# A hybrid encoder block: an SSM scan in three levels, the meta keys' low parts from PSUM, and a reordered end of the experts

## The chip, the cores and the metric

The kernel runs on one core of one Trainium2 chip. The metric is the device time of one execution, in microseconds (us). TensorE (PE) does the matrix products, VectorE (DVE) and ScalarE (ACT) the elementwise work, GpSimd (POOL) some of it too; SyncE (SP), ACT and POOL issue the transfers (DMAs).

## The reference, cut to what matters

One block over 2048 tokens and 16 meta tokens of 1024 values. Attention and a bidirectional state-space layer run side by side, are gated and summed; then come 16 experts that each choose 256 tokens.

```python
q, k, v, u, g_attn, g_ssm = split(layer_norm(concat(meta, x)) @ w_in)
# attention: softmax(q k^T / 8) v over all 2064 keys, 8 heads
# state-space layer, per direction (forward, backward):
s[t] = a * s[t-1] + B u[t]          # a, s complex; 32 groups of 64 states
y[t] = Re(C s[t]) + d * u[t]
y_ssm = glu(gelu(y))
h = layer_norm(alpha * h + (sig(g_attn) * (y_attn @ wa) + sig(g_ssm) * (y_ssm @ ws)) @ w_o)
# experts: each takes its top 256 tokens
moe[idx[e]] += gate[e] * ((silu(xe @ w_gate[e]) * (xe @ w_up[e])) @ w_down[e])
out = layer_norm(alpha * h + moe)
```

## The kernel before

Where precision asks for it, a float32 operand is split into a high part (a copy in a format that TensorE multiplies fast) and a low part (the rest), and a product is three products. The parts are made on the way: high by ACT, low by DVE or POOL.

**Order of the program.** `phase_a` normalises and projects q, k, v and u. Then `ssm` and `glu` run as generators: at each `yield` the driver (`drive`) takes so many steps from `gates`, whose step is four matmuls of 512 columns (L1169). So the gates' products fill TensorE while the state-space layer keeps the other engines busy, and every engine gets its instructions in the order in which the program writes them. A gate weight arrives as `gwr`, ACT makes `gwh`, DVE makes `gwl` (L1127), and the finished gate tile `pg` is read by ACT (L1140).

**`ssm`.** It first loads its parameters: raw `a` (L712), `log_dt` (L714), `c` (L720) and `b` (L724), all from SP's queue. `v_item` computes, per chunk of 16 time steps, what the chunk adds to the state, and ACT copies it to `VA`, a tile with 130 places of 64 values a partition. `scan` then walks over 127 places: five DVE instructions of 64 values for each (L675), the forward and the backward direction in one instruction, from two places of `VA`. Each step takes one gate step. Beside it `k_item` prepares the output weights of five groups; its elementwise instructions are on POOL here (L879, L881). `y_item` multiplies the states by these weights (L1013).

**Attention** goes over 32 units (four blocks of 512 queries by 8 heads). A unit has nine steps `i`: eight of 256 keys and the last, i = 8, of the 16 meta keys. In each step TensorE makes the scores `pS` (L483, L484), ACT the exponential `pe` (L490) and the high part `ph` (L502; for i = 3 DVE, L500), POOL the low part `pl` (L508), and TensorE the product with v (`po`, L525, L527). For the meta keys the low part is made by DVE (L511), from `pe` and `ph` in SBUF. TensorE also makes the scores of the next unit's maxima (`pm`, L449), two at a time, and DVE reduces each (`mx`, L455). After a block's eighth head POOL sends `y` to DRAM (L548).

**Experts.** Each has eight units of gate and up products (`pg`, L1721) and eight of down products (`pd`, L1749), with 24 matmuls of 256 columns in a down unit and 48 in a gate-and-up unit, 9216 in all for 16 experts. From expert 9 on (`E0`) side generators run one step per unit: `finish` normalises rows of the sum that no expert of the end touches, `redo(e - 1)` those of the expert before. `MO` holds their times: at which unit `redo` is started, how many units it waits, the same for the last expert's, and the pitch of `finish`. `norm` takes two row tiles: sums on ACT (L1810, L1816), Newton steps on DVE, then two DVE instructions of 1024 values per tile (L1821, L1822). `put_rows` (L1825) writes rows to the output.

Of the kernel before, what the change touches and what calls it, by code (L numbers as in the profile page):

```python
# [49 lines left out]
def kernel(ctx, tc, x, meta, ln_in_g, ln_in_b, w_in, q_norm_g, k_norm_g,  # L50
# [321 lines left out]
    def phase_b(c):  # L372
# [100 lines left out]
        def scores(n, i, a):  # L473
# [13 lines left out]
            e = pp.tile([128, 2, 512], F32, name="pe", bufs=PR["PE"])  # L487
# [5 lines left out]
        PR = dict(HI=(3,), LOV=(16,), LAG=4, LEAD=3.75, PE=7, PH=5, LOS=2,  # L493
# [98 lines left out]
        for s in range(len(steps) + LAG):  # L592
# [76 lines left out]
    def ssm(c):  # L669
# [7 lines left out]
        VA = tb.tile([128, 2, 32, CB + 2], F32, name="VA")  # L677
        PL.memset(VA[:, 1, :, CB:CB + 1], 0.0)
# [4 lines left out]
        st = tb.tile([128, 2, 2, 32], F32, name="st")  # L683
# [17 lines left out]
        with pool(name="s_i", bufs=1) as ti:  # L701
# [163 lines left out]
            do(V.tensor_scalar, lt[64:, 1], lt[64:, 1], -1.0, None, op0=OP.mult)  # L865
# [7 lines left out]
        up = c1.enter_context(pool(name="s_u", bufs=2))  # L873
        bstv = bst.rearrange("p r (d g) h -> p r d g h", d=2)
# [26 lines left out]

        def v_item(k, d, g):
# [15 lines left out]
            A.copy(VA[:, d, 4 * k + g, :CB], pv[:, :CB])  # L918

        load_u(0, True)  # L920
        make_ws(0)
        yield
        for i, _ in enumerate(pipe(v_item(k, d, g) for k in range(8) for d in range(2) for g in range(4))):
            yield (i + 1) % 2
        c1.close()
        c1 = ExitStack()
        kp = c1.enter_context(pool(name="s_k", bufs=1))
        up = c1.enter_context(pool(name="s_v", bufs=2))
        CL, MM = {}, {}
# [30 lines left out]
        def load_mm(k):  # L960
            mm = kp.tile([128, KT, 2, TH], F32, name="mm", bufs=3)
# [648 lines left out]
    def experts(c, pos, inf):  # L1610
# [446 lines left out]
```

## Time and profile before

| what | value |
|---|---|
| time, median of 3 runs | 3305.42 us (3301.82 to 3309.93) |
| time of the profiled execution | 3306.01 us |
| its span, first to last instruction | 3303.9 us |
| TensorE busy | 92% of the span |
| VectorE busy | 69% |
| ScalarE busy | 47% |
| GpSimd busy | 30% |
| mean granted TensorE clock | 0.966 |

The shares of busy time are means over stages that differ. By the stretches of the span: `phase_a` to 302 us, the state-space layer and gates to 966 us (its scan from 471.6 to 695), attention to 1650 us, merge, router and top-k to 2109 us, experts to the end. The granted clock is a share of full speed (2.4 GHz).

### The profile page before, as it was taken

The numbers are of one execution on the slowest core, as the hardware profiler recorded it, in microseconds if no ns is written. First come the engines' busy times: TensorE is split into PE (matmuls) and PEld (weight loads), VectorE is DVE, ScalarE is ACT, GpSimd is POOL, SyncE is SP. The second block draws the span as 40 slices with busy tenths as digits, with TensorE's granted clock in tenths as the row PEclk, the third lists the DMA queues.
The fourth block names the chain that finished last, engine by engine and source line by source line (L and its number), as shares of the span: only waits on it lengthen the run. The fifth ranks groups of instructions, "written<-read, shape, count | busy, mean of one in ns | idle before, by whom it ended". The sixth has DMA issues, their size and how long they took to land. (4 is left out here: it accounts for less than half of the span.)

```text
span 3303.9 us, 56603 instructions
## 1 busy us (share of the span) xinstructions
PE 3045.8 (92%) x22805; PEld 2686.9 (81%) x22805; DVE 2287.5 (69%) x4206; ACT 1557.3 (47%) x2197; POOL 1000.7 (30%) x633
## 2 busy tenths in 40 slices
PE   6999996788999999999999997599999999999997
PEld 5887785566777777777778886599999999999997
DVE  7884779985357777777556665666566665778875
ACT  2222341112349889898732222344444444556552
POOL 3221050033039989898820001000011001112221
PEclk9999998899999999999999998799999999999998
DMA  6666521544730101012086652366666666878773
GB/s 223 192 193 213 132 77 53 163 131 139 217 109 21 33 21 33 17 36 86 27 254 191 175 169 104 110 210 203 204 205 214 208 204 217 262 235 281 262 255 133
DMA packets 464502, 513.03 MB, mean 155 GB/s; under 512 B 47568, under 2 KB 387728, under 8 KB 463856
## 3 DMA queue, kind: packets, MB, share of 16 engines
q1 hardware_dynamic: 435104, 422.31, 40.4%
q0 software_dynamic: 19232, 69.53, 7.2%
q10 hardware_dynamic: 9904, 17.57, 1.5%
q8 instruction: 179, 2.93, 0.4%
q14 instruction: 83, 0.68, 0.1%
HBM read 385.59 MB, written 123.76 MB: 154 GB/s over the span
## 5 line engine op out<-in xcount | busy, mean ns | idle before, releaser
L1721 PE MATMUL pg<-xh,wh 128*128 128x256 f32 x2048 | 586.3, 286 | 15.7 <-DVE sg L1729 9.7
L1721 PE MATMUL pg<-xh,wl 128*128 128x256 f32 x2048 | 582.8, 285 | 0.5 <-DVE wl L1630 0.5
L1721 PE MATMUL pg<-xl,wh 128*128 128x256 f32 x2048 | 582.9, 285 | 0.0
L1630 DVE TENSOR_TENSOR wl<-wr,wh 128x2048 fp32r<-128x2048 f32 x189 | 433.1, 2292 | 215.1 <-ACT wh L1629 215.1
L508 POOL TENSOR_TENSOR pl<-pe,ph 128x1024 f16<-128x1024 f32 x256 | 554.6, 2201 | 79.7 <-DVE ph L500 67.1
L455 DVE TENSOR_REDUCE mx<-pm 128x1 f32<-128x412 f32 (+1 forms) x640 | 365.5, 584 | 153.6 <-PE pm L449 138.3
L1721 PEld LDWEIGHTS pg<-xh,wh 128*128 128x128 f32 x2048 | 396.6, 194 | 17.0 <-issue 12.2
L1721 PEld LDWEIGHTS pg<-xh,wl 128*128 128x128 f32 x2048 | 396.6, 194 | 0.7 <-DVE wl L1630 0.7
L1721 PEld LDWEIGHTS pg<-xl,wh 128*128 128x128 f32 x2048 | 396.8, 194 | 0.0
L1629 ACT CAST wh<-wr 128x2048 fp32r<-128x2048 f32 x189 | 358.4, 1896 | 7.3 <-DMA wr<-in_w_up_e_dram 5.7
L1169 PE MATMUL pg<-gh,gwh 128*128 128x512 f32 x1024 | 344.8, 412 | 12.9 <-ACT gg L1140 6.9
L490 ACT ACTIVATE pe<-pS,ebias 128x1024 f32<-128x1024 f32 (+1 forms) x288 | 306.6, 1065 | 63.3 <-PE pS L484 62.6
L1749 PE MATMUL pd<-wh,hh 128*128 128x256 f32 x1024 | 292.6, 286 | 5.2 <-ACT ye L1767 2.7
L1749 PE MATMUL pd<-wh,hl 128*128 128x256 f32 x1024 | 290.5, 284 | 0.7 <-DVE hl L1736 0.7
L1749 PE MATMUL pd<-wl,hh 128*128 128x256 f32 x1024 | 290.2, 283 | 0.0
L1169 PE MATMUL pg<-gh,gwl 128*128 128x512 f32 x512 | 213.0, 416 | 63.0 <-DVE gwl L1127 62.9
L449 PE MATMUL pm<-k,q 128*128 128x412 f32 (+1 forms) x640 | 237.7, 381 | 33.4 <-DVE mx L455 29.0
L502 ACT CAST ph<-pe 128x1024 f16<-128x1024 f32 (+1 forms) x256 | 254.2, 993 | 18.3
L1169 PEld LDWEIGHTS pg<-gh,gwh 128*128 128x128 f32 x1024 | 200.1, 198 | 59.8 <-ACT gg L1140 8.8
L525 PEld LDWEIGHTS <-ph 128*128 128x128 f16 (+1 forms) x2176 | 190.5, 97 | 65.0 <-issue 61.8
L525 PE MATMUL po<-v,ph 128*128 128x129 f16 (+1 forms) x2176 | 234.0, 222 | 0.7 <-ACT t L533 0.7
L483 PE MATMUL pS<-q,k 128*128 128x512 f32 (+1 forms) x544 | 232.7, 428 | 0.0
(412 smaller groups left out, 6848.7 us busy)
## 6 DMA issues: line engine op xcount, KB each, us to landing
wr<-in_w_gate_e_dram SPq DMA_DIRECT2D x64, 1024.0 KB
wr<-in_w_up_e_dram SPq DMA_DIRECT2D x64, 1024.0 KB
wr<-in_w_down_e_dram SPq DMA_DIRECT2D x64, 1024.0 KB
gwr<-in_w_in_dram SPq DMA_DIRECT2D x32, 512.0 KB
gh<-ht_d SPq DMA_DIRECT2D x64, 256.0 KB
gt_d<-gg ACTq DMA_DIRECT2D x64, 256.0 KB
gt<-gt_d SPq DMA_DIRECT2D x32, 512.0 KB
q<-q_d SPq DMA_DIRECT2D x96, 128.0 KB
```

The source lines that it names most:

```text
L449: PE.matmul(p[:, :w], Q[n][0][:, 128 * j:128 * j + 128], K1[units[n][1] // 4][:, k0:k0 + w], start=True, stop=True)
L455: V.tensor_reduce(MX[n][:, j, c:c + 1], p[:, :w], axis=AX.X, op=OP.max)
L483: PE.matmul(p[:m, a], K2[g][:, k0:k0 + m], Q[n][1], start=True, stop=False)
L490: A.activation(e[:m, :w], p[:m, :w], AF.Exp, bias=ebias[:m], scale=HD ** -0.5)
L502: A.copy(hi[:m, :w], e[:m, :w])
L508: PL.tensor_tensor(lo[:m, :w], e[:m, :w], hi[:m, :w], op=OP.subtract)
L525: PE.matmul(o[:, 0:129], hi[:m, a, 128 * j:128 * j + 128], v16[:m, kt, g, 0:129], start=(kt == 0 and j % 2 == 0), stop=False, skip_group_c ...
L1169: PE.matmul(p, w[:, k], h, start=(k == 0 and j == 0), stop=(k == 7 and j == 2))
L1629: A.copy(wh, wr)
L1630: V.tensor_tensor(wl, wr, f(wh), op=OP.subtract)
L1721: PE.matmul(p[:, gu], w[:, k, cs_], x[:, k], start=(k == 0 and j == 0), stop=(k == 7 and j == 2))
L1749: PE.matmul(p, a[:, k, cs_], w[:, k], start=(k == 0 and j == 0), stop=(k == 7 and j == 2))
```

## The change

Four parts of the program change.

1. **Attention.** For the meta keys the exponential is written to the free half of the score tile in PSUM (`p[:, 1:]`), and not to a tile in SBUF. DVE's low part reads that. It enters DVE's queue at the end of its own step i = 8, where before it came two steps later with POOL's.
2. **State-space layer.** Nine of the parameter loads are issued by ACT and not by SP. `VA` is laid out place by place, the backward direction in reverse order, so that both directions walk the same way; `powers` makes the first eight powers of `a`. `scan` has three levels: inside 16 segments of 8 places all segments at once (7 steps of 1024 values), then over the segments' ends (15 steps of 64 values), then the ends' contribution to the other places, three segments at once (5 steps of 1344 values). Its wide instructions take two gate steps each. `take_vs` copies a group's states to a contiguous tile for the products; `u` and `mm` of the output stage lie in pools that are opened when the scan is over.
3. **Experts' memory.** A pad of 32 bytes stands ahead of the experts' tiles and one of 64 bytes ahead of the token tiles `xh`, `xl`, which get a pool of their own.
4. **Experts' order.** 24 transposes of a constant stand ahead of the first gather's use. In the last seven experts `MO` is (2, 5, 5, 11), the two long DVE instructions of `norm` are a step apart, `finish` loads its next rows earlier, and the last expert's down units finish the first half of its rows earlier.

```diff
@@ attention
-            e = pp.tile([128, 2, 512], F32, name="pe", bufs=PR["PE"])
+            e = pp.tile([128, 2, 512], F32, name="pe", bufs=PR["PE"]) if w == 2 else p[:, 1:]
...
+        def split_lo(n, i):
             e, hi, lo, m, w = P[n, i]
...
+            (PL if w == 2 else V).tensor_tensor(lo[:m, :w], e[:m, :w], hi[:m, :w], op=OP.subtract)
...
-                vq += split_lo(*steps[s - PR["LOS"]], True)
+            if 0 <= s - PR["LOS"] < len(steps) and steps[s - PR["LOS"]][1] < NP - 1:
+                split_lo(*steps[s - PR["LOS"]])
...
                 split_hi(n, i, False)
+                if i == NP - 1:
+                    vq.insert(0, lambda st=steps[s]: split_lo(*st))
@@ ssm
-        VA = tb.tile([128, 2, 32, CB + 2], F32, name="VA")
+        VA = tb.tile([128, CB + 1, 2, 32], F32, name="VA")
...
-                    SP.dma_start(raw[:, i, j], src.rearrange("l d g p -> (l d g) p"))
+                    A.dma_start(raw[:, i, j], src.rearrange("l d g p -> (l d g) p"))
...
-            SP.dma_start(ldt, row_bcast(ssm_log_dt, DG))
+            A.dma_start(ldt, row_bcast(ssm_log_dt, DG))
...
-                    SP.dma_start(craw[:, :, x, y], src.rearrange("l d g h p -> (l d g h) p")
+                    A.dma_start(craw[:, :, x, y], src.rearrange("l d g h p -> (l d g h) p")
...
-            A.copy(VA[:, d, 4 * k + g, :CB], pv[:, :CB])
+            dst = VA[:, 1:, d, 4 * k + g]
+            A.copy(back(dst, CB) if d else dst, pv[:, :CB])
...
+        def take_vs(k):
+            VS[k] = yp.tile([128, 2, 2, CX], F32, name="vs", bufs=2)
+            for d in range(2):
+                src = VA[:, 1 - d:1 - d + CX, d, 2 * k:2 * k + 2]
+                A.copy(VS[k][:, d].rearrange("p g c -> p c g"), back(src, CX) if d else src)
...
-            for m in range(1, CB - 1):
-                f0, f1 = m - 1, m
-                b0, b1 = CB - m, CB - 1 - m
-                tt(st[:, 0], lt[:, 0], slot(f0, b0, 0, 128), OP.mult)
-                tt(st[:64, 1], lt[64:, 1], slot(f0, b0, 64, 128), OP.mult)
-                tt(st[64:, 1], lt[:64, 1], slot(f0, b0, 0, 64), OP.mult)
-                cur = slot(f1, b1, 0, 128)
-                tt(cur, cur, st[:, 0], OP.add)
-                tt(cur, cur, st[:, 1], OP.add)
+            for j in range(1, SL):
+                dims = [NS, 64]
+                coef = [wide(z[:, r, 0:1], dims) for r in range(2)]
+                for _ in step(coef, v[:, j - 1], v[:, j], dims):
+                    yield 2
+            for s in range(1, NS):
+                for _ in step([z[:, r, SL - 1] for r in range(2)], v[:, SL - 1, s - 1], v[:, SL - 1, s], [64]):
+                    pass
+                yield
+            B = 3
+            for s in range(1, NS, B):
+                dims = [B, SL - 1, 64]
+                coef = [wide(z[:, r, None, 0:SL - 1], dims) for r in range(2)]
+                prev = wide(v[:, SL - 1, s - 1:s - 1 + B, None], dims)
+                cur = v[:, 0:SL - 1, s:s + B].rearrange("p j s x -> p s j x")
+                for _ in step(coef, prev, cur, dims):
+                    yield 2
...
-        kk = pipe((k_item(k, False) for k in range(5)), every=22)
+        kk = pipe((k_item(k, False) for k in range(5)), every=12)
...
+        up = c1.enter_context(pool(name="s_v", bufs=2))
+        yp = c1.enter_context(pool(name="s_y", bufs=3))
@@ experts
+        c.enter_context(pool(name="e_pad", bufs=1)).tile([128, 8], F32, name="skew")
...
-        MO = dbg.get('MO', (2, 6, 3, 11)) if dbg else (2, 6, 3, 11)
+        MO = dbg.get('MO', (2, 5, 5, 11)) if dbg else (2, 5, 5, 11)
...
+        c.enter_context(pool(name="e_skew", bufs=1)).tile([128, 16], F32, name="skew")
+        tp = c.enter_context(pool(name="e_xt", bufs=2))
...
-                    put_rows(e, h)
+                    if h:
+                        put_rows(e, h)
...
                 V.scalar_tensor_tensor(x, x, mean[:, j:j + 1], gb, op0=OP.add, op1=OP.mult)
+                yield
                 V.scalar_tensor_tensor(x, x, r[:, j:j + 1], bb, op0=OP.mult, op1=OP.add)
...
-                yield from norm([xs[t], xs[t + 1]])
+                for n, _ in enumerate(norm([xs[t], xs[t + 1]])):
+                    if n == 7 and t + 2 < NT:
+                        load(t + 2)
+                        load(t + 3)
+                    yield
...
-            yield from norm(AC[e])
-            put_rows(e, 0)
-            yield
-            yield
+            for n, _ in enumerate(norm(AC[e])):
+                if n == 7:
+                    put_rows(e, 0)
+                yield
             put_rows(e, 1)
...
-        pick_out(0, pick(0))
+        pi = pick(0)
+        for _ in range(3):
+            p = pp.tile([128, 4, 128], F32, name="pt")
+            for k in range(8):
+                PE.transpose(p[:, k % 4], idf, idf)
+        pick_out(0, pi)
...
+            seq = [(i, h) for i in range(4) for h in range(2)]
+            if not more:
+                seq[4:] = [(2, 0), (3, 0), (2, 1), (3, 1)]
...
+        put_rows(E - 1, 0)
         run(post)
```

How the rows stand on the engines is seen at three places. On DVE, between two units of the attention, before (`mx` are the maxima, `nm` what is made of a unit's twenty, L511 the meta keys' low part):

```order
L464 TENSOR_REDUCE nm_8226<-m_8652 128x4
L455 TENSOR_REDUCE mx<-pm 128x1 x10
L511 TENSOR_TENSOR pl<-pe,ph 16x512
L455 TENSOR_REDUCE mx<-pm 128x1 x7
L500 TENSOR_REDUCE ph<-pe 128x1024
```

And with the change, where L506 is the same low part, read from the score tile in PSUM:

```order
L464 TENSOR_REDUCE nm_7900<-m_8286 128x4
L455 TENSOR_REDUCE mx<-pm 128x1 x8
L506 TENSOR_TENSOR pl<-pS,ph 16x512
L455 TENSOR_REDUCE mx<-pm 128x1 x9
L500 TENSOR_REDUCE ph<-pe 128x1024
```

The low part has moved ahead by two maxima, and its first operand is PSUM.

On DVE at the start of the scan, before (the last rows of the input weights `ws`, then the first two places of the scan; `gwl` belongs to the gates):

```order
L881 TENSOR_TENSOR ws<-ws,wt 128x1024
L675 TENSOR_TENSOR st<-lt,VA 128x64
L675 TENSOR_TENSOR st<-lt,VA 64x64 x2
L675 TENSOR_TENSOR VA<-VA,st 128x2x32 x2
L675 TENSOR_TENSOR st<-lt,VA 128x64
```

And with the change at the same place:

```order
L894 TENSOR_TENSOR ws<-ws,wt 128x1024
L1009 TENSOR_TENSOR st_5058<-pw,VA 128x1024
L1011 TENSOR_TENSOR st_5059<-pw,VA 64x1024
L1188 TENSOR_TENSOR gwl<-gwr,gwh 128x1024
L1013 TENSOR_TENSOR st_5059<-pw,VA 64x1024
L1015 TENSOR_TENSOR VA<-VA,st_5058 128x16x64
L1017 TENSOR_TENSOR VA<-VA,st_5059 128x16x64
L1009 TENSOR_TENSOR st_5125<-pw,VA 128x1024
```

635 short rows became 35 of 1024 values, 75 of 64 and 25 of 1344; the `gwl` rows, 11 before and 11 now, stand between the wide ones.

On ACT at the start of the state-space layer, before (L251 ends `phase_a`; L1140 reads a finished gate tile, L1141 sends it away):

```order
L251 CAST qh<-pk 128x16
L1140 ACT_TABLE_LOAD
L1140 ACTIVATE gg<-pg 128x512
L1141 DMA gt_d<-gg 128x512
L1140 ACTIVATE gg<-pg 128x512
```

And with the change:

```order
L251 CAST qh<-pk 128x16
L708 DMA s_3480<-in_ssm_a_re_dram 64x64 x2
L708 DMA s_3480<-in_ssm_a_im_dram 64x64 x2
L710 DMA s_3485<-in_ssm_log_dt_dram 128x64
L716 DMA s_3488<-in_ssm_c_re_dram 128x8x64
L716 DMA s_3488<-in_ssm_c_im_dram 128x8x64 x2
L716 DMA s_3488<-in_ssm_c_re_dram 128x8x64
L1201 ACT_TABLE_LOAD
L1201 ACTIVATE gg<-pg 128x512
```

The nine loads now stand ahead of ACT's first reading of a gate tile.

## Rows read from the trace of the kernel before

**Rows 1.** Windows: length, busy (count) PE, PEld, DVE, ACT, POOL, clock, DMA, GB/s

```profile
395.00:471.60 76.60, 76.34 (x530) 69.53 (x529) 58.68 (x51) 45.65 (x139) 25.74 (x31) 1.00 0.35 105
471.60:695.00 223.40, 158.12 (x595) 119.25 (x593) 205.65 (x656) 30.61 (x45) 28.91 (x24) 0.84 0.33 105
```

**Rows 2.** DVE's groups by line in the scan: busy us, mean ns, idle before

```profile
L675 DVE TENSOR_TENSOR st<-lt,VA 128x64 f32<-128x64 f32 x381 | 115.7, 304 | 19.9 <-ACT VA L918 10.5
L675 DVE TENSOR_TENSOR VA<-VA,st 128x64 f32<-128x64 f32 x254 | 76.7, 302 | 8.3
L1127 DVE TENSOR_TENSOR gwl<-gwr,gwh 128x1024 fp32r<-128x1024 f32 x11 | 14.3, 1298 | 0.0
```

**Rows 3.** Waits in the scan: us in total, times, longest

```profile
PE pg L1169 <- DVE gwl L1127: 62.4, 10, 13.9
```

**Rows 4.** DVE in order of time, early in the scan: start, us, what

```profile
489.30 2.14 DVE L1127 TENSOR_TENSOR gwl<-gwr,gwh 128x1024 fp32r<-128x1024 f32 x1
```

**Rows 5.** POOL in order of time, same stretch

```profile
490.32 2.09 POOL L879 TENSOR_TENSOR ct<-lo_t,cst 128x544 f32<-128x544 f32 x1
...
499.77 1.36 POOL L881 TENSOR_TENSOR cl<-cl,ct 128x544 f32<-128x544 f32 x1
```

**Rows 6.** DVE's groups by line and shape, whole span

```profile
L511 DVE TENSOR_TENSOR pl<-pe,ph 16x512 f16<-16x512 f32 x32 | 95.7, 2989 | 5.9 <-ACT ph L502 5.9
L1709 DVE TENSOR_TENSOR xl<-pt,xh 128x512 fp32r<-128x512 f32 x64 | 41.2, 683 | 7.9 <-ACT xh L1708 7.8
L879 DVE TENSOR_TENSOR ws<-go_t,bst 128x1024 f32<-128x1024 f32 x16 | 19.6, 1223 | 2.4 <-PE pA L909 1.8 <-POOL bbar L899 0.6
```

**Rows 7.** Waits of PE in the attention: us in total, times, longest

```profile
PE pm L449 <- DVE mx L455: 28.7, 28, 5.8
```

**Rows 8.** DVE in order of time at the end of a block of queries

```profile
1319.63 8.02 DVE L511 TENSOR_TENSOR pl<-pe,ph 16x512 f16<-16x512 f32 x1
```

**Rows 9.** POOL in order of time, same stretch

```profile
1312.40 14.71 POOL L508 TENSOR_TENSOR pl<-pe,ph 128x1024 f16<-128x1024 f32 x7
```

**Rows 10.** Windows: a unit of attention, and one at a block's end

```profile
1208.00:1228.10 20.10, 19.55 (x197) 15.48 (x194) 15.42 (x28) 18.18 (x21) 18.49 (x11) 1.00 0.07 22
1138.90:1168.20 29.30, 23.43 (x198) 18.48 (x195) 20.93 (x28) 18.21 (x21) 20.27 (x13) 0.83 0.15 50
```

**Rows 11.** ACT in order of time: the first exponential of a unit

```profile
1216.22 1.11 ACT L490 ACTIVATE pe<-pS,ebias 128x1024 f32<-128x1024 f32 x1 [0.37 <-PE pS L484]
```

**Rows 12.** PE in order of time: the same unit's second scores

```profile
1216.91 0.48 PE L483 MATMUL pS<-q,k 128*128 128x512 f32 x1
```

**Rows 13.** SP's queue in order of time, at the state-space layer's start

```profile
309.80 18.42 SPq L1134 DMA_DIRECT2D gh<-ht_d  x16
328.80 2.08 SPq L712 DMA_DIRECT2D s<-in_ssm_a_re_dram  x2
...
335.65 1.15 SPq L720 DMA_DIRECT2D s<-in_ssm_c_re_dram  x1
```

**Rows 14.** PE in order of time, same stretch

```profile
320.86 1.06 PE L1169 MATMUL pg<-gh,gwh 128*128 128x512 f32 x2 [1.62 <-DMA gh<-ht_d]
```

**Rows 15.** Waits of PE in the experts

```profile
PE pg L1721 <- DVE sg L1729: 9.7, 3, 6.3
PE pg L1721 <- DVE iv L1674: 5.4, 2, 4.4
```

**Rows 16.** ACT in order of time in the last expert

```profile
3243.28 1.06 ACT L1810 ACTIVATE fj<-fa 128x1024 f32<-128x1024 f32 x1 [10.31 <-DMA fa<-acc_d,ix]
...
3245.70 1.06 ACT L1810 ACTIVATE fj<-fa 128x1024 f32<-128x1024 f32 x1 [1.28 <-DMA fa<-acc_d,ix]
```

**Rows 17.** PE's matmuls of 256 columns, by line and shape

```profile
L1721 PE MATMUL pg<-xh,wh 128*128 128x256 f32 x2048 | 586.3, 286 | 15.7 <-DVE sg L1729 9.7 <-DVE iv L1674 5.4 <-DVE xl L1709 0.5
L267 PE MATMUL pu<-hth,wh 128*128 128x256 f32 x256 | 71.3, 279 | 1.3 <-ACT wh L156 1.3
```

**Rows 18.** PE in order of time, at the first gather

```profile
2103.64 1.97 PE L1699 MATMUL pt<-idf,xg 128*128 128x128 f32 x8 [9.50 <-DMA xg<-h_d,ix]
```

More of the change, by code (lines that the diff above doesn't have):

```diff
@@ L873, in ssm, with powers @@
         up = c1.enter_context(pool(name="s_u", bufs=2))
+        cw = ExitStack()
+        wp = cw.enter_context(pool(name="s_w", bufs=1, side="right"))
+        pw = wp.tile([128, 2, SL, 64], F32, name="pw")
+        pt = wp.tile([128, 2, SL // 2, 64], F32, name="pt")
+        def powers():
+            V.tensor_copy(pw[:, :, 0], lt.rearrange("p r d g -> p r (d g)"))
+            n = 1
+            while n < SL:
+                a, b = [pw[:, r, n - 1:n].to_broadcast([128, n, 64]) for r in range(2)]
+                for x0, x1, o, op in ((0, 1, 0, OP.subtract), (1, 0, 1, OP.add)):
+                    V.tensor_tensor(pt[:, 0, :n], pw[:, x0, 0:n], a, op=OP.mult)
+                    V.tensor_tensor(pt[:, 1, :n], pw[:, x1, 0:n], b, op=OP.mult)
+                    V.tensor_tensor(pw[:, o, n:2 * n], pt[:, 0, :n], pt[:, 1, :n], op=op)
+                    yield
+                n *= 2
+            V.tensor_scalar(pw[64:, 1], pw[64:, 1], -1.0, None, op0=OP.mult)
         bstv = bst.rearrange("p r (d g) h -> p r d g h", d=2)
@@ L900, in make_ws, with back @@
             WS[i] = ws
+        def back(a, n):
+            (step, _), off = a.ap[1], a.offset
+            return bass.AP(tensor=a.tensor, offset=off + step * (n - 1),
+                           ap=[list(a.ap[0]), [-step, n]] + [list(z) for z in a.ap[2:]])
         def v_item(k, d, g):
@@ L960, in load_mm @@
         def load_mm(k):
-            mm = kp.tile([128, KT, 2, TH], F32, name="mm", bufs=3)
+            mm = yp.tile([128, KT, 2, TH], F32, name="mm", bufs=3)
             for g in range(2):
@@ L987, in ssm, with scan, step, wide @@
-        kk = pipe((k_item(k, False) for k in range(5)), every=22)
-        for _ in scan():
-            next(kk, None)
-            yield
+        def scan(sp):
+            v = VA[:, 1:1 + CX].rearrange("p (s j) d g -> p j s (d g)", j=SL)
+            z = pw
+            def step(coef, prev, cur, dims):
+                shape = [128] + dims
+                s0, s1 = [sp.tile([128, math.prod(dims)], F32, name=f"st{i}") for i in range(2)]
+                if len(dims) > 1:
+                    names = " ".join("abc"[:len(dims)])
+                    kw = dict(zip("abc", dims))
+                    s0, s1 = [t.rearrange(f"p ({names}) -> p {names}", **kw) for t in (s0, s1)]
+                V.tensor_tensor(s0, coef[0], prev, op=OP.mult)
+                yield
+                V.tensor_tensor(s1[:64], coef[1][64:], prev[64:], op=OP.mult)
+                yield
+                V.tensor_tensor(s1[64:], coef[1][:64], prev[:64], op=OP.mult)
+                yield
+                V.tensor_tensor(cur, cur, s0, op=OP.add)
+                yield
+                V.tensor_tensor(cur, cur, s1, op=OP.add)
+                yield
+            def wide(a, dims):
+                return a.to_broadcast([128] + dims)
+            for j in range(1, SL):
[5 more added lines that the diff above has]
+                for _ in step([z[:, r, SL - 1] for r in range(2)], v[:, SL - 1, s - 1], v[:, SL - 1, s], [64]):
+                    pass
+                yield
+            B = 3
[6 more added lines that the diff above has]
+                    yield 2
@@ L991, in ssm @@
+        kk = pipe((k_item(k, False) for k in range(5)), every=12)
+        with pool(name="s_c", bufs=2) as sp:
+            for r in scan(sp):
+                next(kk, None)
+                yield r
+        cw.close()
+        up = c1.enter_context(pool(name="s_v", bufs=2))
+        yp = c1.enter_context(pool(name="s_y", bufs=3))
+        for k in range(2):
+            take_vs(k)
         for _ in kk:
```

56 lines of the change are left out of this document (21 added, 35 removed).

## The prediction

> **What bounds the kernel now.** I read the windows by stage first, since TensorE's 92% is a mean over stages. While the input weights of the state-space layer are made, TensorE is busy for 76.34 of 76.6 us. In the scan it is busy for 158.12 of 223.4 us at a granted clock of 0.84, and DVE for 205.65 [rows 1]: the scan is DVE's stage. DVE's groups there show with what: 635 instructions of 64 values take 115.7 + 76.7 = 192.4 us, 0.303 us each, beside 14.3 us for the gates' `gwl` [rows 2]. The waits show how this reaches TensorE: the gates' matmuls wait ten times for `gwl`, 62.4 us in all [rows 3], since `gwl` stands in DVE's queue behind the scan's rows.
>
> In the attention a unit takes 20.1 us with TensorE busy for 19.55; at a block's end one takes 29.3 with a clock of 0.83 [rows 10]. The waits of PE name DVE's maxima: 28 waits, 28.7 us, the longest 5.8 [rows 7]. The last number is not like the mean, so I looked at DVE's row at such a place: the meta keys' low part, 16 x 512 values, takes 8.02 us [rows 8], while POOL runs seven of its own low parts back to back, 14.71 us [rows 9]. The same DVE form takes 2.989 us on average over 32 units [rows 6]. The maxima are late because they queue behind it.
>
> In the experts TensorE works without a break except in the last seven, where it waits 9.7 us for `sg` and 5.4 us for `iv`, both DVE's [rows 15].
>
> **Part 1, meta keys in PSUM.** The low part no longer has two SBUF operands, and the nearest row with one operand in PSUM and one in SBUF is 128 x 512 in 0.683 us [rows 6]. I take that for L506, 2.3 us less than the mean of L511, and 7.3 less at a block's end. There are three such ends inside the attention. Three waits of 5.8 are 17.3 of the 28.7 us; the other 25 waits share 11.4, about 0.45 each. At an end I count the whole unit, since the half clock behind the pause goes too: 29.3 - 20.1 = 9.2, three times 27.6. POOL still sends `y` there and is late with its own low parts; I take 26. The ordinary waits give 11 more.
>
> Against that stands a new wait. The score tile of i = 8 is now read until L506 is done, which moves the order in which the pool hands out score tiles: the second score tile of the next unit gets the buffer of the first, so its matmul must wait for that tile's exponential. Before, the exponential ran from 1216.22 to 1217.33 [rows 11] and the second scores began at 1216.91 [rows 12], so 0.42 us are lost, 31 times: 13 us. It all comes to -26 - 11 + 13 = **-24 us**. Bounds: -38 if the new wait is hidden, -8 if POOL's lateness at the block's end takes the pause's place and only a third of it goes.
>
> **Part 2, the scan.** The nearest row for 1024 values is 1.223 us [rows 6]. From 0.303 for 64 values that is 0.96 ns a value, so 1344 values take 1.53 us (an estimate from these two). The new rows cost 35 x 1.223 = 42.8, 75 x 0.303 = 22.7 and 25 x 1.53 = 38.3, in all 103.8 where 192.4 stood. With the rest of DVE's stage, 205.65 - 192.4 = 13.3 us, `gwl` almost alone, DVE has 117 us.
>
> Next is late what POOL does at the same time. Its 24 instructions of the scan take 28.9 us [rows 1] and run without a break until 501 [rows 5]. Beside them a DVE instruction of 1024 values with two SBUF operands took 2.14 us [rows 4] where the same group's mean is 1.298 [rows 2], and POOL's own took 2.09 in the place of some 1.2 [rows 5]. So each wide row beside POOL loses 0.9 us, 24 times 22 us: DVE needs 139 us. The Trainium skill ("SBUF — State Buffer", Who interferes with whom) states that a DVE instruction with two SBUF inputs contends with a GpSimd instruction that reads SBUF, and that one blocks the other for the whole instruction. The two rows agree with it; by a rule without such a lock the stage would need 22 us less.
>
> TensorE's share of the stage doesn't change: 138 gate steps before, 70 + 15 + 50 = 135 now. Its work at full clock is 158.12 x 0.84 = 133 us. Two engines with 139 and 133 us that hand work to each other don't overlap fully; before, 223.4 - 205.65 = 18 us of the stage were not DVE's, 8%. I take 139 + 8% and some more for the first wide rows, 153 us, a gain of **70 us**. Bounds: 133 (TensorE alone, -90), and 183 (-40), if the rows with a repeated operand take a quarter longer than the plain ones. The powers of `a` are some 20 small DVE rows in the stage before, where DVE is busy for 58.68 of 76.6 us [rows 1], hidden; without the cover some 6 us. The copies to `VA` now step over 64 values at each value, and the 32 new copies in `take_vs` are ACT's: ACT is busy for 45.65 of 76.6 and 30.61 of 223.4 us [rows 1], so they cost nothing unless the output stage waits for the first of them; that is inside the bounds. The loads of `u` and `mm`, which now wait for the end of the scan, lie beside ten gate steps (138 take 133 us).
>
> **Part 2, the loads.** Nine loads leave SP's queue, where they took from 328.80 to 336.80, and stand on ACT ahead of the first reading of a gate tile [rows 13]. SP issues 16 loads of `gh` between 309.80 and 328.22 [rows 13], 1.15 us each, since each waits until an earlier one has landed. ACT's loads wait for landings of the same row, so ACT may stand until 328 to 333, and with it the gate tile's reading. What is queued behind: the matmuls of the next gate tiles, which began at 320.86 [rows 14]. The loss is between the issue alone (7 us, less the 1.62 that PE waited for `gh` anyway) and 14 us. SP's next loads, of `b` and of a gate weight, come 8 us sooner, which gives back up to 3.4 us. I take **+6 us**, bounds 0 and +14.
>
> **Part 3, the pads.** They move addresses only. Nothing in the profile ties an address to a duration: matmuls of 256 columns have a mean of 286 ns in the experts and 279 ns in `phase_a` [rows 17], and I could not see why. I take 0. Bounds: 7 ns on 9216 matmuls either way, 65 us.
>
> **Part 4, the experts' order.** In the last expert ACT waits 10.31 us for the gathered rows [rows 16] and with it the silu of a finished tile, and TensorE 6.3 us for `sg` [rows 15]. ACT had stood there since 3243.28 - 10.31 = 3232.97. `MO` starts this `norm` two units later, and a unit of 48 matmuls takes some 6 us (9216 matmuls in the experts' 1195 us): at 3245, where the first rows have landed (3243.28) and the second lack 1 us (3245.70) [rows 16]. So 6.3 us and the half clock behind them go, 7 in all. The 4.4 us for `iv` come from three pairs of long DVE rows at once, which now stand a unit apart: -4. What is late next: the moved `norm` of the last expert ends in the last unit, its 1.28 us rows between the last outputs, and three row writes go out together; +3 to +4. Earlier loads in `finish` don't help its first pair, whose wait stays. The transposes fill 9.50 us in which TensorE waited for the gather at half clock [rows 18]; the following matmuls then begin at full clock: -2. In all **-10 us**, bounds -17 and +2.
>
> **The sum.** -24 - 70 + 6 - 10 = -98. Against the profiled execution's 3306.0 us (0.6 over the median of the runs) that is 3208 us.
>
> **Rivals.** First, POOL keeps the scan's gain. At the end of a block of queries the DVE row did not take turns with POOL: it lasted through three or four POOL instructions, 8.02 us [rows 8]. If the wide rows fare so, DVE stands for POOL's whole 28.9 us [rows 1] and the stage's overlap suffers: with TensorE waiting for `gwl` at half clock the gain falls from 70 to some 30, 3248 us. For it speaks the row of 8.02; against it that `gwl` in the same stretch took 2.14 [rows 4].
>
> Second, the pads move the matmuls. If the experts' 286 ns become the 279 of `phase_a` [rows 17], 65 us more go: 3143 us. For it speaks only that the two rows differ.
>
> Third, on the other side: the pads slow the matmuls. At +7 ns the change would still gain 33 us; it loses from 98/9216 = 10.6 ns a matmul on, and at 12 ns, 111 us, the time would be 3319. No row shows a matmul of 256 columns so slow at full clock, which speaks against it.
>
> Fourth, the meta keys' change gives nothing: if POOL's own lateness at the block's end ends last, only 8 of the 24 us come, 3224 us, and if the loads also cost their upper bound, 3232. Inside the range.
>
> **Chances and range.** The forecast with its bounds, 3175 to 3240: 0.76. The first rival, 3240 to 3290: 0.12. The second, under 3175: 0.07. The third, or several terms wrong at once: 0.05, of which 0.03 slower. The range that leaves out two in ten reaches from 3175 to 3260. 0.3% (10 us) is what a measurement of this kernel can tell from no change; faster by more has 0.95, the same 0.02, slower 0.03.
>
> **What the profile after would show.** Right: a scan stage of 145 to 160 us from the first L1009 to the last L1017, with wide rows near 1.2 us once POOL's are done and near 2.1 beside them; no PE wait of 5.8 us for maxima, units at block ends under 22 us, and a short wait of the second scores for the exponential; ACT standing between its two loads and the first gate tile until about 330; no `sg` wait of 6 us in the last expert. Wrong: wide rows above 1.6 us without POOL beside them, PE waiting for POOL's `pl` at block ends, experts' matmuls with another mean than 286 ns, or waits that the scan's end hands to the first output products.

## The result and the profile after

The changed kernel takes 3186.28 us (median of 4 runs, 3182.40 to 3190.51), the kernel before 3305.73 in the same comparison: a ratio of 0.9639, 95% interval 0.9622 to 0.9656. The change takes off 119 us; 98 were forecast. The profiled execution has a span of 3180.6 us, 123.3 less than before. By the starts and ends of each stage's matmuls the 123.3 us lie here (the scan's start is the end of the last matmul ahead of it):

| stage | change, us | forecast, us |
|---|---|---|
| start of the state-space layer to the scan's start | +8.4 | +6 |
| scan, to the first output product | -72.4 | -70 |
| output products (127.8 to 123.5) | -4.3 | 0 |
| from there to the attention | +1.1 | 0 |
| attention (664.1 to 634.8) | -29.3 | -24 |
| merge, router, top-k, first gather | +0.6 | -2 (transposes) |
| experts 0 to 8 (647.2 to 633.4) | -13.8 | 0 (pads) |
| experts 9 to 15, to the last matmul (533.1 to 515.0) | -18.1 | -11 |
| from the last matmul to the end (14.3 to 18.7) | +4.4 | +3 |

The windows of the profile after (columns as in [rows 1]): the stage ahead of the scan, the scan's stage with the ten gate steps behind its last row, the scan alone, and a unit of attention at the end of a block of queries.

```profile
404.80:479.70 74.90, 74.08 (x518) 67.79 (x517) 61.27 (x68) 45.95 (x136) 21.96 (x30) 1.00 0.34 101
...
479.70:629.30 149.60, 146.89 (x624) 112.97 (x624) 134.18 (x157) 33.32 (x52) 48.77 (x24) 0.99 0.48 150
...
480.00:620.00 140.00, 137.29 (x582) 105.06 (x581) 132.95 (x156) 29.63 (x45) 48.47 (x24) 0.99 0.48 147
...
1070.40:1090.30 19.90, 19.52 (x198) 15.67 (x195) 13.61 (x28) 18.06 (x21) 17.87 (x12) 1.00 0.24 74
```

In the scan's stage TensorE is now busy for 146.89 of 149.6 us at a clock of 0.99, where [rows 1] have 158.12 of 223.4 at 0.84; DVE is busy for 134.18, and in the scan alone for 132.95 of 140 us. Both engines are nearly full; which of them holds the other, the run with half the gate steps tells. The unit at a block's end takes 19.9 us, where [rows 10] have 29.3, and its clock doesn't fall.

DVE's groups in the scan of the kernel after (busy us, mean ns, idle before); L1009 to L1017 are the five rows of a step, in three sizes:

```profile
L1188 DVE TENSOR_TENSOR gwl<-gwr,gwh 128x1024 fp32r<-128x1024 f32 x12 | 17.7, 1475 | 3.9 <-ACT gwh L1187 3.6
L1017 DVE TENSOR_TENSOR VA<-VA,st 128x1024 f32<-128x1024 f32 x7 | 12.6, 1804 | 0.2
...
L1009 DVE TENSOR_TENSOR st<-pw,VA 128x1344 f32<-128x1344 f32 x5 | 7.7, 1549 | 0.0
...
L1009 DVE TENSOR_TENSOR st<-pw,VA 128x64 f32<-128x64 f32 x15 | 3.3, 222 | 0.4
```

The 1344 values take 1.55 us (1.53 were estimated), the 64 values 0.222 (0.303 were taken). The mean of 1.804 for 1024 values mixes two kinds, which the order of time shows, DVE early in the scan and later:

```profile
486.15 2.03 DVE L1013 TENSOR_TENSOR st<-pw,VA 64x1024 f32<-64x1024 f32 x1
488.21 2.03 DVE L1015 TENSOR_TENSOR VA<-VA,st 128x1024 f32<-128x1024 f32 x1
490.27 2.27 DVE L1017 TENSOR_TENSOR VA<-VA,st 128x1024 f32<-128x1024 f32 x1
...
532.48 1.22 DVE L1011 TENSOR_TENSOR st<-pw,VA 64x1024 f32<-64x1024 f32 x1
```

And POOL in the first of these stretches:

```profile
485.00 2.10 POOL L892 TENSOR_TENSOR cl<-lo_t,cst 128x544 f32<-128x544 f32 x1
487.06 2.10 POOL L892 TENSOR_TENSOR ct<-lo_t,cst 128x544 f32<-128x544 f32 x1
489.23 2.23 POOL L894 TENSOR_TENSOR cl<-cl,ct 128x544 f32<-128x544 f32 x1
```

While POOL works, the two engines take turns at one row each per 2.1 us, and both rows look long. From 530 us on, with POOL done, DVE's row takes 1.22. The first rival (POOL runs through and DVE stands) didn't come.

At the start of the state-space layer, ACT of the kernel after:

```profile
316.95 3.39 ACTq L708 DMA_DIRECT2D s<-in_ssm_a_re_dram  x2
...
329.49 0.91 ACTq L716 DMA_DIRECT2D s<-in_ssm_c_re_dram  x1
330.43 1.28 ACT L1201 ACT_TABLE_LOAD   x1 [14.24 <-DMA s<-in_ssm_c_im_dram]
331.73 0.60 ACT L1201 ACTIVATE gg<-pg 128x512 f32<-128x512 f32 x1
```

And PE's next gate tiles:

```profile
332.38 1.22 PE L1230 MATMUL pg<-gh,gwh 128*128 128x512 f32 x2 [13.57 <-ACT gg L1201]
```

ACT stands 14.24 us over its nine loads, which it issues from 316.95 to 330.40 us; the matmuls that began at 320.86 [rows 14] begin at 332.38.

PE's waits in the attention of the kernel after, and DVE's row for the meta keys:

```profile
PE pS L483 <- ACT pe L490: 9.2, 30, 0.3
PE pm L449 <- DVE mx L455: 2.2, 3, 1.5
```

```profile
L506 DVE TENSOR_TENSOR pl<-pS,ph 16x512 f16<-16x512 f32 x32 | 21.4, 670 | 14.7 <-ACT ph L502 14.7
```

The row takes 0.670 us (0.683 were taken from an equal one). The waits for maxima, 28.7 us in [rows 7], are 2.2, and the new wait of the second scores for the first exponential is there, 30 times, 0.31 us each.

In the experts, PE's matmuls by line and shape, after:

```profile
L1785 PE MATMUL pg<-xh,wh 128*128 128x256 f32 x2048 | 574.6, 281 | 5.6 <-DVE sg L1793 4.9 <-DVE xl L1773 0.5 <-DVE iv L1738 0.2
L1785 PE MATMUL pg<-xh,wl 128*128 128x256 f32 x2048 | 571.7, 279 | 1.0 <-DVE wl L1692 1.0
...
L1813 PE MATMUL pd<-wh,hh 128*128 128x256 f32 x1024 | 293.2, 286 | 4.8 <-ACT ye L1832 2.9 <-DVE ye L1819 1.9
```

The gate-and-up matmuls have the 279 ns of `phase_a` [rows 17], the down matmuls still 286. From the first matmul of an expert to that of the next it was 71.74 us in most of the first nine; now it is 69.65 or 70.9.

POOL at the end of the kernel after:

```profile
3164.73 0.97 POOL L1891 DMA_INDIRECT out_dram<-fa,io  x1 [7.89 <-DVE fa L1888]
3168.32 1.92 POOL L1891 DMA_INDIRECT out_dram<-ye,io  x1 [2.62 <-DMA out_dram<-fa,io]
3173.36 0.95 POOL L1891 DMA_INDIRECT out_dram<-ye,io  x1 [3.12 <-DMA out_dram<-ye,io]
```

The last write waits for the landing of the one ahead, and that for the one ahead of it.

### The profile page after: what moved, and what is told of

It is laid out like the page before. It is cut to its first block, busy times and chain, and to the rows that moved or that the text cites. A ratio compares the mean times of both kernels' runs of the same rounds, so it can differ in the third digit from the quotient of the medians.

```text
span 3180.6 us, 56184 instructions
## 1 busy us (share of the span) xinstructions
PE 3000.1 (94%) x22829; PEld 2654.5 (83%) x22829; DVE 2146.7 (67%) x3725; ACT 1571.6 (49%) x2229; POOL 1011.9 (32%) x633
## 4 chain that ended last, share of the span: by engine, by line
PE 61%; DVE 14%; ACT 8%; DMA 7%; issue 6%; POOL 3%; SPq 1%; ACTq 0%; POOLq 0%; DVEq 0%
PE pg L1785 17%; PE pd L1813 8%; PE pg L1230 6%; PE pw L1383 5%; PE pb L1315 5%; PE pm L449 3%; PE pS L483 3%; ACT pe L490 2%; PE pS L484 2%; PE po L520 2%; DVE wl L1692 2%; POOL pl L506 1%; PE pz L1147 1%; DVE ph L500 1%; DMA gh<-ht_d 1%
## 5 line engine op out<-in xcount | busy, mean ns | idle before, releaser
L1785 PE MATMUL pg<-xh,wh 128*128 128x256 f32 x2048 | 574.6, 281 | 5.6 <-DVE sg L1793 4.9
L1785 PE MATMUL pg<-xh,wl 128*128 128x256 f32 x2048 | 571.7, 279 | 1.0 <-DVE wl L1692 1.0
L1785 PE MATMUL pg<-xl,wh 128*128 128x256 f32 x2048 | 571.5, 279 | 0.0
L506 POOL TENSOR_TENSOR pl<-pe,ph 128x1024 f16<-128x1024 f32 x256 | 542.4, 2149 | 59.9 <-DVE ph L500 49.1
L1785 PEld LDWEIGHTS pg<-xh,wl 128*128 128x128 f32 x2048 | 386.1, 189 | 1.7 <-DVE wl L1692 1.6
L1785 PEld LDWEIGHTS pg<-xl,wh 128*128 128x128 f32 x2048 | 386.2, 189 | 0.0
L1230 PE MATMUL pg<-gh,gwh 128*128 128x512 f32 x1024 | 333.2, 401 | 21.1 <-ACT gg L1201 17.5
L490 ACT ACTIVATE pe<-pS,ebias 128x1024 f32<-128x1024 f32 x256 | 284.8, 1112 | 37.9 <-PE pS L484 37.9
L502 ACT CAST ph<-pe 128x1024 f16<-128x1024 f32 x224 | 234.4, 1047 | 15.6
L522 PE MATMUL po<-v,pl 128*128 128x65 f16 (+1 forms) x2176 | 220.2, 192 | 2.2 <-POOL pl L506 2.1
```

Source lines behind the costliest of these rows:

```text
L490: A.activation(e[:m, :w], p[:m, :w], AF.Exp, bias=ebias[:m], scale=HD ** -0.5)
L502: A.copy(hi[:m, :w], e[:m, :w])
L506: (PL if w == 2 else V).tensor_tensor(lo[:m, :w], e[:m, :w], hi[:m, :w], op=OP.subtract)
L1230: PE.matmul(p, w[:, k], h, start=(k == 0 and j == 0), stop=(k == 7 and j == 2))
L1785: PE.matmul(p[:, gu], w[:, k, cs_], x[:, k], start=(k == 0 and j == 0), stop=(k == 7 and j == 2))
```

## Experiments

Each kernel is the changed one with the edit shown, unless the text says otherwise; `...` marks lines left out. Times are medians, beside 3186.3 us for the changed kernel; ratios are to the kernel before, beside 0.9639 (0.9622 to 0.9656). The intervals of several single edits overlap with that one; for these the stage in the trace decides.

**Without the pads.**

```diff
-        c.enter_context(pool(name="e_pad", bufs=1)).tile([128, 8], F32, name="skew")
...
-        c.enter_context(pool(name="e_skew", bufs=1)).tile([128, 16], F32, name="skew")
-        tp = c.enter_context(pool(name="e_xt", bufs=2))
...
-                XT[e] = (tp.tile([128, 8, CAP], F32R, name="xh"), tp.tile([128, 8, CAP], F32R, name="xl"))
+                XT[e] = (xp.tile([128, 8, CAP], F32R, name="xh"), xp.tile([128, 8, CAP], F32R, name="xl"))
```

> The changed kernel without the two pads: xh and xl lie in the pool of the other token tiles again, and leave the same remainder by 128 bytes as the weights. Theory P (the pads made the gate-and-up matmuls start closer together): the 6144 matmuls start 120 ns apart again, as before the change, and no longer 113 to 119; some 28 us of the gain go, 3214 us. Rival R (the experts' gain of 32 us comes from their new order): 3186 us as with the pads.

Measured: 3200.66 us, ratio 0.9682 (0.9662 to 0.9702). Its order of time on PE, in an expert's gate-and-up part:

```profile
2400.07 0.28 PE L1782 MATMUL pg<-xl,wh 128*128 128x256 f32 x1
2400.19 0.28 PE L1782 MATMUL pg<-xh,wl 128*128 128x256 f32 x1
2400.31 0.28 PE L1782 MATMUL pg<-xh,wh 128*128 128x256 f32 x1
```

The matmuls start 120 ns apart again and an expert takes 71.74 us: theory P holds for where the 14 us come from. But P's 28 us were twice too many. Experts 0 to 8 take 647.3 us without pads and 633.4 with them; the last seven take 514.4 and 515.0. Of the last seven, with the pads and then without:

```profile
2646.90:3161.90 515.00, 500.77 (x4322) 496.49 (x4320) 390.12 (x683) 286.80 (x382) 106.27 (x83) 0.99 0.76 249
```

```profile
2660.80:3175.20 514.40, 505.06 (x4322) 501.51 (x4320) 390.58 (x683) 286.47 (x382) 105.89 (x83) 1.00 0.77 249
```

There the shorter matmuls turn into waits: TensorE's add up to 14.2 us with the pads and 9.4 without, most of it for DVE (`sg` 4.9 for 2.1, `xl` 2.7 for 0.3), and the clock is 0.99 for 1.00.

**Only the pad of 64 bytes.**

```diff
-        c.enter_context(pool(name="e_pad", bufs=1)).tile([128, 8], F32, name="skew")
```

> The changed kernel with the pad of 64 bytes ahead of the token tiles, without the one of 32 bytes ahead of everything. Weights lie at remainder 64 by 128, xh and xl at 0, so the difference is 64 as with both pads. Theory P1 (the difference between the two operands' addresses counts): 113 to 119 ns, 3186 us. Rival P2 (the place of the weights themselves counts, which the 32 bytes moved): 120 ns, 3214 us.

Measured: 3187.76 us, ratio 0.9635 (0.9617 to 0.9653); gate-and-up matmuls of 279 to 281 ns. The 32 bytes do nothing that these runs can tell. So the weights' own place, rival P2, isn't what counts. By remainder of 128 bytes the token tiles lie at 0 here and at 32 with both pads, each time 64 from the weights, which speaks for the distance; their own place wasn't tested apart from it.

**The hidden tiles set apart too.**

```diff
-                HT[e] = (xp.tile([128, 8, CAP], F32R, name="hh", bufs=1), xp.tile([128, 8, CAP], F32R, name="hl", bufs=1))
+                HT[e] = (tp.tile([128, 8, CAP], F32R, name="hh", bufs=1), tp.tile([128, 8, CAP], F32R, name="hl", bufs=1))
```

> The changed kernel with the hidden tiles hh and hl in the pool behind the 64 bytes as well, so that the down matmuls' operands differ by 64 too. Theory P1: the 3072 down matmuls, 120 ns apart until now, start 113 to 119 ns apart, 116 in the mean; 3072 x 4 ns = 12 us less, 3174 us. Rival P2, or a bound of the down matmuls of its own: 120 ns and 3186 us.

Measured: 3177.77 us, ratio 0.9609 (0.9591 to 0.9627). PE's down matmuls in this kernel:

```profile
L1813 PE MATMUL pd<-wh,hh 128*128 128x256 f32 x1024 | 288.6, 282 | 6.1 <-ACT ye L1832 3.8 <-DVE ye L1819 2.1
...
L1813 PE MATMUL pd<-wl,hh 128*128 128x256 f32 x1024 | 285.9, 279 | 0.0
```

They shorten as the gate-and-up matmuls did, and 8.5 us go, not 12: again only the first nine experts gain (625.7 us for 633.4; the last seven take 516.3).

**Other distances.** `xh`, `xl` 128 bytes from the weights by remainder of 256, `hh`, `hl` 32 bytes.

```diff
-        c.enter_context(pool(name="e_skew", bufs=1)).tile([128, 16], F32, name="skew")
+        c.enter_context(pool(name="e_skew", bufs=1)).tile([128, 8], F32, name="skew")
+        hp = c.enter_context(pool(name="e_h", bufs=1))
+        c.enter_context(pool(name="e_skew2", bufs=1)).tile([128, 24], F32, name="skew2")
...
-                HT[e] = (xp.tile([128, 8, CAP], F32R, name="hh", bufs=1), xp.tile([128, 8, CAP], F32R, name="hl", bufs=1))
+                HT[e] = (hp.tile([128, 8, CAP], F32R, name="hh", bufs=1), hp.tile([128, 8, CAP], F32R, name="hl", bufs=1))
```

> The changed kernel with other distances: xh and xl 128 bytes apart from the weights (by remainder of 256), hh and hl 32 bytes. Theory P1 with a remainder by 128: gate-and-up matmuls 120 ns apart again, down matmuls below 120. Rival with a larger remainder (256 and more): gate-and-up matmuls stay at 113 to 119. A third reading, that only 64 bytes do it: down matmuls at 120. By the first 3186 + 14 - 8 = 3192 us.

Measured: 3191.22 us (2 runs), ratio 0.9651 (0.9634 to 0.9669). All three readings fail: gate-and-up matmuls have 282 to 284 ns and down matmuls 282 to 285, between the two kinds; that the time is the 3192 us of the first reading is chance. Any distance that was tried helps, 64 bytes most. What the distance does is not settled.

**Loads on SP again.**

```diff
-                    A.dma_start(raw[:, i, j], src.rearrange("l d g p -> (l d g) p"))
+                    SP.dma_start(raw[:, i, j], src.rearrange("l d g p -> (l d g) p"))
```

and so for the other two.

> The changed kernel with the nine parameter loads issued by SP again. Theory L (ACT stood behind its own loads, and TensorE 13.57 us behind ACT's reading of the gate tile): that wait goes, the first rows of the scan start some 8 us sooner, 3178 us. Rival (the loads' data come as much later from SP, and DVE's parameter rows begin no sooner): 3186 us.

Measured: 3177.81 us, ratio 0.9610 (0.9593 to 0.9627), 8.5 us less. ACT's first gate tile and PE's next matmuls in this kernel:

```profile
318.57 0.60 ACT L1201 ACTIVATE gg<-pg 128x512 f32<-128x512 f32 x1
```

```profile
319.48 1.08 PE L1230 MATMUL pg<-gh,gwh 128*128 128x512 f32 x2 [0.89 <-DMA gh<-ht_d]
```

Theory L holds: ACT reads the tile at 318.57, not at 331.73, and TensorE waits 0.89 us in the place of 13.57.

**The meta keys' exponential in SBUF, at the new place in the queue.**

```diff
-            e = pp.tile([128, 2, 512], F32, name="pe", bufs=PR["PE"]) if w == 2 else p[:, 1:]
+            e = pp.tile([128, 2, 512], F32, name="pe", bufs=PR["PE"])
```

> The changed kernel with the meta keys' exponential in an SBUF tile again; the low part stays on DVE and keeps its new, earlier place in the queue. Theory B (two SBUF operands beside POOL's low parts made the row long): L506 takes some 2.7 us in ordinary units and 8 at a block's end again, three units of about 29 us return, the wait of the second scores for the first exponential (9.2 us) goes; the attention loses 20 to 29 us, 3206 to 3215 us. Rival O (the place in the queue was what counted): the units stay at 19.9 us or fall by the 0.3 us of that wait, 3177 to 3186 us.

Measured: 3214.50 us, ratio 0.9727 (0.9710 to 0.9743), 28 us more. DVE's group and a row at a block's end, then PE's waits:

```profile
L506 DVE TENSOR_TENSOR pl<-pe,ph 16x512 f16<-16x512 f32 x32 | 96.6, 3017 | 14.9 <-ACT ph L502 14.9
```

```profile
1082.19 8.02 DVE L506 TENSOR_TENSOR pl<-pe,ph 16x512 f16<-16x512 f32 x1
```

```profile
PE pm L449 <- DVE mx L455: 31.8, 31, 5.8
```

Theory B holds entirely: mean 3.017 us, 8.02 at a block's end, the waits of 5.8 us. The new place in the queue is worth nothing by itself. The Trainium skill ("SBUF — State Buffer", Who interferes with whom) states that a DVE instruction with two SBUF inputs contends with a GpSimd instruction that reads SBUF, and that one with at most one, outside the 2-port modes, doesn't. The two kernels agree, with 3.017 and 0.670 us for the same row.

**One gate step for each wide row.**

```diff
-                    yield 2
+                    yield 1
```

and so at the second place.

> The changed kernel with one gate step, not two, for each wide row of the scan, so that 60 of the 135 gate steps (54 us of TensorE) are done later. Theory E (TensorE is the bound of the new scan, busy for 146.9 of its 149.6 us): the scan's stage falls to what DVE needs, 125 to 132 us, and the 54 us come back where the rest of the gates runs, 3215 to 3225 us. Rival D (DVE beside POOL is the bound, as the prediction had it): the stage loses only the 7 us of the missing gwl rows, 142 us, and the time is 3230 to 3235 us.

Measured: 3230.86 us (2 runs), ratio 0.9772 (0.9751 to 0.9793). The stage, DVE's group of `gwl` rows in it, and the first output product of this kernel:

```profile
479.70:614.00 134.30, 99.42 (x378) 69.53 (x376) 128.28 (x152) 21.62 (x37) 50.62 (x26) 0.86 0.33 110
...
L1188 DVE TENSOR_TENSOR gwl<-gwr,gwh 128x1024 fp32r<-128x1024 f32 x7 | 10.5, 1498 | 0.1
...
622.10 0.38 PE L1069 MATMUL pB<-u,mm 128*128 128x128 f32 x2
```

DVE's scan lasts from 482.1 to 612.9 us, 131 us against 140 with two steps, and the stage to the first output product 140 us against 149.6. Of these 9 us 7 are DVE's own: it has 7 rows of `gwl` here (10.5 us) and 12 in the changed kernel (17.7). With 60 gate steps less beside it DVE's scan is faster by only 2 us more. So theory D holds: DVE beside POOL bounds the scan, 142 us and 3230 to 3235 were expected by it. Theory E's 125 to 132 us are met by DVE's rows but not by the stage, and its total isn't met. The 9 us are lost again in the output products, which end at 752.4 us here and at 752.8 in the changed kernel, and the gates come later by 57 us. TensorE stands right behind DVE in the changed kernel, with 137.29 us in the scan's 140.

**The last norm unsplit.**

```diff
-                yield
+                if split:
+                    yield
...
-            for n, _ in enumerate(norm(AC[e])):
-                if n == 7:
+            for n, _ in enumerate(norm(AC[e], e < E - 2)):
+                if n == (7 if e < E - 2 else 6):
```

> The changed kernel with the two long rows of norm side by side again in the last expert's redo alone, so that the writes of expert 14's rows are issued one and two units sooner. Theory W (the end is 4.4 us longer from the last matmul on because three writes of rows to the output stand one behind the other): the last write is issued as soon as DVE's last row is done, the end after the last matmul falls from 18.7 to some 15 us, 3182 to 3184 us. Rival (DVE's rows between the last outputs cause it): no change, 3186 us.

Measured: 3180.86 us, ratio 0.9625 (0.9607 to 0.9643). POOL at its end:

```profile
3158.38 0.97 POOL L1892 DMA_INDIRECT out_dram<-fa,io  x1 [3.15 <-DVE lst L1822]
3162.57 0.95 POOL L1892 DMA_INDIRECT out_dram<-ye,io  x1 [3.23 <-DVE ye L1828]
3168.38 0.95 POOL L1892 DMA_INDIRECT out_dram<-ye,io  x1 [4.86 <-DVE ye L1828]
```

The writes wait for DVE alone, and the end after the last matmul is 14.6 us (3175.6 - 3161.0), 4.1 less: theory W. The medians differ by 5.4 with overlapping intervals; the trace decides.

**`finish` one unit later.**

```diff
             for t in range(2):
                 load(t)
             yield
             yield
+            yield
```

> The changed kernel with one more unit between finish's first loads and its first sums. Theory F (ACT stands 9.13 us for the first rows fx in expert 9 and TensorE 4.9 us behind it): the wait of ACT falls to 3 us, TensorE's goes with the half clock behind it, 5 to 7 us less, 3180 us. Rival (the later pairs fall on the redo's sums and cost as much elsewhere): 3186 us.

Measured: 3178.04 us, ratio 0.9617 (0.9600 to 0.9634). ACT at the first sums, in the changed kernel and in this one:

```profile
2676.25 1.06 ACT L1875 ACTIVATE fj<-fx 128x1024 f32<-128x1024 f32 x1 [9.13 <-DMA fx<-acc_d]
```

```profile
2674.68 1.06 ACT L1875 ACTIVATE fj<-fx 128x1024 f32<-128x1024 f32 x1 [3.18 <-DMA fx<-acc_d]
```

ACT's wait falls to 3.18 us and TensorE's of 4.9 us is gone; from the first to the last expert matmul 6.4 us go (1148.4 to 1142.0). Theory F holds, though expert 14's unit grew from 72.4 to 78.3 us: part of it came back there, as the rival said.

**The four edits together:** loads on SP, hidden tiles set apart, last norm unsplit, `finish` one unit later.

> The changed kernel with four edits that were each run alone: the loads on SP again (8.5 us less there), the hidden tiles behind the 64 bytes too (8.5), norm unsplit in the last expert (5.4), finish one unit later (8.2). Theory S (they cost in different places: start of the state-space layer, experts 0 to 8, the end, expert 9): the sum holds, 30.6 us less than 3186.3, 3156 us. Rival (the last seven experts are bound by DVE and ACT, so the edits there eat each other's gain): the first two and half of the others, 3162 to 3166 us.

Measured: 3154.62 us (5 runs, 3154.33 to 3160.43), ratio 0.9546 (0.9533 to 0.9559). The sum holds. This is the fastest version here: 151 us below the kernel before, 32 below the changed one.

**And operands of 512 columns set apart.**

```diff
+        c.enter_context(pool(name="g_skew", bufs=1, side="right")).tile([128, 16], F32, name="skew")
         wp = c.enter_context(pool(name="g_w", bufs=2, side="right"))
+        c.enter_context(pool(name="o_skew", bufs=1)).tile([128, 8], F32, name="skew")
         sb = c.enter_context(pool(name="m_s", bufs=1))
```

> The kernel with four edits, and the operands of two groups of matmuls of 512 columns set apart as well: the gates' by 64 bytes (1536 matmuls), the output projection's by 32 (768). Theory P1 (operands with the same remainder cost each matmul some 4 ns): 226 to 227 ns become 220 to 224 and 6 to 9 us go, 3147 to 3150 us. Rival (the 4 ns are a matter of the short matmuls, whose weights load in the time of 256 columns): 226 ns and the time of the four edits.

Measured: 3159.85 us, ratio 0.9557 (0.9542 to 0.9573), not faster. PE's groups, in the kernel with the four edits and then in this one:

```profile
L1230 PE MATMUL pg<-gh,gwh 128*128 128x512 f32 x1024 | 331.9, 399 | 11.4 <-ACT gg L1201 5.5 <-DMA gh<-ht_d 4.1 <-ACT gwh L1187 1.6
...
L1383 PE MATMUL pw<-woh,mh 128*128 128x512 f32 x256 | 103.7, 405 | 0.0
```

```profile
L1231 PE MATMUL pg<-gh,gwh 128*128 128x512 f32 x1024 | 334.3, 401 | 12.6 <-ACT gg L1202 5.7 <-DMA gh<-ht_d 5.0 <-ACT gwh L1188 1.7
...
L1385 PE MATMUL pw<-woh,mh 128*128 128x512 f32 x256 | 104.7, 409 | 0.0
```

Theory P1 fails for matmuls of 512 columns: 64 bytes apart they are no shorter (401 ns for 399; the changed kernel, without that pad, has 401 too), 32 bytes apart 4 ns longer.

## Why the prediction was right

**The scan: right in size and in its bound, two terms off.** The price per row held (1.22 and 1.55 us for 1.223 and 1.53, 2.0 to 2.3 beside POOL for 2.14), and the stage took 149.6 us where 153 were forecast. DVE bounds it, as forecast; it needs 134.18 us and not 139, since the 75 rows of 64 values take 0.222 us each and not 0.303, 6 us less. The 0.303 was a mean of two kinds: of the rows of L675 the first 23, beside POOL, take 26.96 us, and the 613 from 501.1 us on take 165.24, 0.27 each. What the rest, 0.27 to 0.222, comes from wasn't tested.

The step that failed is "TensorE's share of the stage doesn't change: 138 gate steps before, 70 + 15 + 50 = 135 now", and with it "158.12 x 0.84 = 133 us". The gates' matmuls in the stage, before and after:

```profile
L1169 PE MATMUL pg<-gh,gwh 128*128 128x512 f32 x367 | 127.0, 429 | 1.8 <-DMA gh<-ht_d 1.8
L1169 PE MATMUL pg<-gh,gwl 128*128 128x512 f32 x184 | 81.3, 442 | 62.4 <-DVE gwl L1127 62.4
```

```profile
L1230 PE MATMUL pg<-gh,gwh 128*128 128x512 f32 x390 | 123.2, 396 | 2.0 <-DMA gh<-ht_d 2.0
L1230 PE MATMUL pg<-gh,gwl 128*128 128x512 f32 x194 | 76.8, 396 | 0.7 <-DVE gwl L1188 0.7
```

551 matmuls became 584, at four a step 138 and 146 steps: the 138 hold the ten steps behind the scan's last row, and the 135 don't. The 33 matmuls more are some 8 us at 146.89/624 = 0.235 us each. And 0.84 is the clock of the whole stage, the time in which TensorE stood included; where it was busy the granted clock was 0.87, which makes 138 us of the 158.12. 138 + 8 is what was measured, 146.89 us at 0.99. So TensorE was priced 12 us too low and DVE 5 too high, and the allowance for imperfect overlap hid both: that the stage came within 4 us is partly luck.

**The loads: right.** ACT stood until 330, as the text had it, and TensorE lost 13.57 us of which the later stages gave some back; 8.4 measured, 8.5 by the run with SP, 6 forecast. SP's loads of `b` came 4.3 us sooner (332.52 for 336.85) and not 8, since its 16 loads of `gh` took 22.66 us for 18.42. That each of these waits for a landing was said too broadly: in the kernel before, landings of `gh` ended 7 of SP's waits there, 5.5 us.

**The meta keys: right, a little small.** L506 takes 0.670 us; the new wait is real, 9.2 us where 13 were taken; the pauses at the block ends went completely, and POOL was not late there (19.9 us a unit). 29.3 measured, 24 forecast; the smaller wait is most of the difference. The run with SBUF shows the mechanism: two SBUF operands on DVE beside POOL's low parts.

**The pads: the step that failed.** "Nothing in the profile ties an address to a duration ... I take 0." The runs show 14 us. The row was there: 279 ns against 286 in [rows 17], and the second rival had named it. Its price of 65 us was 7 ns on all 9216 matmuls. Only the 6144 of gate and up moved, from 120 ns to some 116 from start to start, and only in the first nine experts, where TensorE is busy without a break, does the time follow: 3456 matmuls at 4 ns are 13.8 us.

**The experts' order: right, with other parts.** Without pads the last seven experts take 514.4 us in the place of 533.1, and the end is 4.4 us longer: -14.3, where -10 were forecast. The wait of 6.3 us for `sg` in the last expert went, as did that of 4.4 for `iv`. The late writes cost 4.4 us, 4.1 by the unsplit run, where 3 to 4 were set down for them. The transposes, forecast at -2, gave nothing. They end before the gather lands, TensorE waits again, and from 2007.8 to 2013.4 us the granted clock is 0.50:

```profile
2007.88 1.94 PE L1763 MATMUL pt<-idf,xg 128*128 128x128 f32 x8 [4.47 <-DMA xg<-h_d,ix]
```

So the step "the following matmuls then begin at full clock" failed; from the pick to the first expert matmul it is 18.2 us, 18.3 before.

Of the 25 us by which the profiled executions differ from the forecast (123.3 against 98) the pads are 13.8, the attention 5.3, the output products 4.3, the order with the transposes 3.1 and the scan 2.4; the loads and the stretch ahead of the attention go 3.5 the other way.

## What to carry to other kernels

A DVE row with two SBUF operands is as long as the POOL rows beside it let it be: here moving one operand to PSUM took 16 x 512 values from 3.0 to 0.67 us, and a queue behind such a row is where to look for pauses that a mean hides. When a stage's bound is taken away, price the second engine as carefully as the first, and count its work in both kernels in the same way: here DVE has 134 us and TensorE 147 in a stage where DVE alone had 205. Two equal forms with different means, 286 and 279 ns here, are a term of the sum until an experiment says otherwise, not a zero.

## What the runs showed of the hardware that I had not expected

Where the two operands of a matmul of 256 columns lie in SBUF changes its pace: 120 ns from start to start with the same remainder by 256 bytes, as the tiles' sizes have it (286 ns a row), 113 to 119 with 64 bytes between (279 to 281), in between with 32 (282 to 285) and 128 (282 to 284). For 512 columns distances of 64 and 32 bytes gave 401 for 399 and 409 for 405 ns. Nine loads issued by ACT while the DMA engines were full (a share of 1.03 from 302 to 338 us) held ACT for 14.24 us. Of three indexed writes to the output tensor the second and the third waited for the landing of the one ahead, 2.62 and 3.12 us. In the scan DVE and POOL took turns row by row; why DVE's row at a block's end lasted through several rows of POOL, 8.02 us, no run shows.
